# Folding the Fourier branch of a token-mixing kernel about the middle of each segment, with its norm in channel-major form and a new order of steps

## The chip, the core and the metric

The kernel is one program on one core of a Trainium2 chip. Its engines are TensorE (PE, matrix products, with PEld its weight loads), VectorE (DVE), ScalarE (ACT), GpSimd (POOL) and SyncE (SP, which issues transfers). The metric is the time of one execution on the device, in microseconds; lower is better.

## The reference

A two-layer block over 512 latent tokens and 256 context tokens of width 1024. Each layer has a token-mixing stage and a SwiGLU stage, each followed by a modulated residual and a layer norm. The mixing stage projects the tokens to three head groups: group A (512 channels, a bidirectional linear recurrence with a GELU gate), group B (256 channels, chunked spatial gating) and group C (256 channels in four heads of 64), which is the Fourier branch that this case is about. Context tokens are a segment of their own, of 256 positions.

```python
def fourier_mix(xf, wf):
    Bsz, L, _ = xf.shape
    z = xf.reshape(Bsz, L, H_C, HEAD_DIM).astype(jnp.float32)
    f = jnp.fft.fft2(z, axes=(1, 3), norm="ortho").real
    return jnp.einsum("blhc,hce->blhe", f, wf.astype(jnp.float32)).reshape(Bsz, L, D_C).astype(xf.dtype)
...
    y = jnp.concatenate([rms_norm(y_a, g_mix[:D_A]),
                         rms_norm(y_b, g_mix[D_A:D_A + D_B]),
                         rms_norm(y_c, g_mix[D_A + D_B:])], -1)
    return y @ w_out
```

The real part of the transform is C z cos - S z sin, with the position matrices C and S on the left and the channel matrices on the right. The last layer needs latent tokens only.

## The kernel before

Tokens lie in tiles of 128: two of context, four of latents (the second layer mixes the four alone). Channel-major buffers hold 128 channels by up to 768 tokens. All large products run on float32r operands: `split` makes a high part on ACT (L208) and a low part by a subtraction (L203) on an engine that the caller chooses, and `mm` multiplies high by high, high by low and low by high, three products in a row on PE. All products are issued by one line, L134. Plain float32 products appear in the profile as two records each.

Weights come in units of mostly 1024 columns (512 KB) in a written order, loaded ahead by SP and split ahead of use; the subtraction of a unit goes to `wsub`, which is POOL at a mixing stage's start and becomes DVE at the letter D of the stage's string; it keeps its value in the MLP that follows. In the MLP PE makes the up projections of one tile of hidden channels after another (L1234 and L1235 in the profile) and, after 4 or 5 of these, the down projection of the group for every token tile; its residual sum ends in an addition on POOL.

The mixing stage follows a string of letters, STEPS, and PE's order is bound to it (`pe.fixed`). Letters that matter here: Z and z load and compute the Fourier input projection (`fourier_in`, split by L877 on ACT and L878 on DVE), c is the column transform (`fourier_cols`), e, p and s are the gates and scans of the recurrence, whose activations fill ACT (L822 to L833), V, v, U, u and t are the spatial gating, g is a gate of group A, m a block of the modulation of later stages (`mod`, with copies at L522), R the rows of the gate, L lets the held GELUs go, a digit sets a memory reserve, D is as above.

After the string, the function `mixing` puts group B's rows (`put_group`: transposes to channel-major), sums group A's squares over channels by products with a column of ones, makes a reciprocal root (`rstd`: DVE, then a power on POOL, L232) and a diagonal matrix from it on DVE (L1172). Then `fourier` computes the positions: for each token tile the products of the full position matrices (units dftc, k_cosl and k_sinl, 4.5 MB over the two layers) with the transformed columns, token-major, a copy and `rms` on ACT and DVE, and a tile later the transposes by `put_group`. Before tile BETWEEN the spread of group A's roots (products with a matrix of ones) and its scaling come in between. The output projection follows, and its layer norm.

## Time and profile before

| | us |
|---|---|
| median of 3 runs | 1506.51 (1502.71 to 1507.05) |
| the profiled execution | 1506.1 |
| its span | 1504.1 |
| PE busy in the span | 1416.7 |
| DVE, ACT, POOL busy | 893.4, 551.7, 294.8 |

From about 60 to 352 us the first layer mixes tokens, up to 860 us its MLP runs; from there to 1139 us the second layer mixes, its MLP ends at 1487 us. A row of the timeline gives the start, the duration, the instruction and, in brackets, the idle time in front of it with the engine and tile that ended it. Ends of products are modelled, so two rows' distance from start to start is the better measure of what products cost.

### The profile page before, as it was taken

What the parts mean: (1) busy time and instruction counts of PE and PEld (TensorE: products, weight loads), DVE (VectorE), ACT (ScalarE), POOL (GpSimd) and SP (SyncE); (2) the same over time, 40 slices, a digit from 0 to 9 for tenths busy, and PEclk for the clock granted to TensorE, in tenths of its full rate; (3) what the DMA queues carried; (4) which work ended last, traced back from release to release, by engine and by line L of the source; (5) the groups of instructions that cost most, each with busy time, mean ns of one, the idle gap of its engine ahead of it and who ended that gap; (6) DMA issues with size and microseconds to landing.
All of it is one profiled execution on the core that took longest, in us unless ns stands there. A gap on an engine that the chain in (4) does not pass through costs nothing.

```text
span 1504.1 us, 18734 instructions
## 1 busy us (share of the span) xinstructions
PE 1416.7 (94%) x7527; PEld 1197.2 (80%) x7527; DVE 893.4 (59%) x1259; ACT 551.7 (37%) x784; POOL 294.8 (20%) x190
## 2 busy tenths in 40 slices
PE   6999888999999999999999998959998999999997
PEld 3788756779888888888888878858777888888885
DVE  6749756779527439443527396688788343353427
ACT  4576445345312202111203146886536232322210
POOL 3303323230021030030030044223230111020201
PEclk9999999999999999999999999969999999999999
DMA  9503365317116216244127004015427352242201
GB/s 329 139 15 99 105 224 186 97 31 236 43 43 211 70 55 198 71 139 162 36 77 231 28 29 128 1 48 169 127 67 228 98 154 71 70 130 60 77 14 56
DMA packets 169430, 163.56 MB, mean 109 GB/s; under 512 B 10456, under 2 KB 126648, under 8 KB 169344
## 3 DMA queue, kind: packets, MB, share of 16 engines
q1 hardware_dynamic: 169232, 162.08, 34.4%
q8 instruction: 59, 0.97, 0.3%
q0 software_dynamic: 112, 0.30, 0.1%
q14 instruction: 27, 0.22, 0.0%
HBM read 160.25 MB, written 2.10 MB: 108 GB/s over the span
## 4 chain that ended last, share of the span: by engine, by line
PE 72%; DVE 12%; ACT 5%; issue 3%; DMA 3%; POOL 3%; SPq 2%; DVEq 0%; POOLq 0%; ACTq 0%
PE mm L134 67%; PE aux L134 5%; POOL smalls L232 2%; DVE f L678 1%; DVE f L203 1%; DVE f L1220 1%; DMA f<-in_w_in_dram 1%; DVE r L203 1%; SPq L1315 1%; POOL r L203 1%; SPq L1333 1%; DVE f L832 1%; DVE smalls L709 1%; ACT r L208 1%; DVE f L835 1%
## 5 line engine op out<-in xcount | busy, mean ns | idle before, releaser
L134 PE MATMUL mm<-r,r 128*128 128x512 f32 (+1 forms) x6192 | 1230.6, 360 | 21.0 <-DVE f L1220 7.3
L134 PEld LDWEIGHTS mm<-r,r 128*128 128x128 f32 x6192 | 1035.7, 191 | 202.0 <-DVE f L1220 12.5
L208 ACT ACTIVATE r<-f 128x1024 fp32r<-128x1024 f32 (+2 forms) x244 | 227.1, 951 | 578.0 <-PE mm L134 267.9
L203 DVE TENSOR_TENSOR r<-f,r 128x1024 fp32r<-128x1024 f32 (+3 forms) x245 | 266.8, 1111 | 133.8 <-ACT r L208 119.9
L203 POOL TENSOR_TENSOR f<-f,f 128x1024 f32<-128x1024 f32 (+2 forms) x44 | 109.7, 2493 | 654.3 <-DVE f L1220 479.3
L1220 DVE TENSOR_TENSOR f<-mm,f 128x512 f32<-128x512 f32 (+1 forms) x80 | 76.2, 952 | 145.2 <-PE mm L134 145.1
L203 POOL TENSOR_TENSOR r<-f,r 128x1024 fp32r<-128x1024 f32 (+2 forms) x59 | 107.0, 1823 | 226.0 <-ACT r L208 159.3
L1235 DVE TENSOR_TENSOR f<-mm,f 128x768 f32<-128x768 f32 (+1 forms) x44 | 36.2, 823 | 176.0 <-PE mm L134 176.0
L134 PE MATMUL aux<-r,r 128*128 128x256 f32 (+1 forms) x780 | 112.5, 306 | 25.3 <-DVE r L878 10.7
L134 PEld LDWEIGHTS aux<-r,r 128*128 128x128 f32 x780 | 106.5, 211 | 32.5 <-DVE r L878 12.7
L232 POOL TENSOR_TENSOR smalls<-smalls,neghalf 128x1 f32<-128x1 f32 (+2 forms) x69 | 67.2, 975 | 255.1 <-DVE smalls L231 245.7
L573 DVE SCALAR_TENSOR_TENSOR f<-f,stc,f 128x512 f32<-128x512 f32 x140 | 102.3, 762 | 2.8 <-DMA f<-in_w_mod_dram 1.3
L203 DVE TENSOR_TENSOR f<-f,f 128x512 f32<-128x512 f32 (+1 forms) x66 | 61.7, 939 | 9.8 <-ACT f L801 8.1
L1234 ACT ACTIVATE f<-mm 128x768 f32<-128x768 f32 (+1 forms) x44 | 30.7, 699 | 95.7 <-PE mm L134 95.7
L134 PE MATMUL aux<-cst,f 128*128 128x128 f32 (+2 forms) x259 | 38.7, 282 | 25.1 <-ACT f L644 8.7
L659 ACT ACTIVATE f<-aux,modT 128x128 f32<-128x128 f32 x128 | 48.5, 466 | 33.3 <-PE aux L134 33.3
L134 PEld LDWEIGHTS aux<-cst,f 128*128 128x128 f32 (+2 forms) x259 | 29.7, 143 | 37.3 <-ACT f L644 11.5
L644 ACT ACTIVATE f<-f,smalls 128x1024 f32<-128x1024 f32 x19 | 23.6, 1242 | 90.8 <-DVE smalls L643 90.8
L777 DVE SCALAR_TENSOR_TENSOR f<-mm,par,f 128x255 f32<-128x255 f32 (+3 forms) x48 | 26.1, 605 | 17.4 <-ACT f L771 17.4
L623 DVE BATCH_NORM_STATS2 smalls<-f 128x6 f32<-128x512 f32 x44 | 28.4, 682 | 5.0 <-DMA f<-in_ctx_dram 4.6
L801 ACT ACTIVATE f<-mm,par 128x768 f32<-128x768 f32 x32 | 28.0, 903 | 6.5 <-PE mm L134 5.0
L832 DVE SCALAR_TENSOR_TENSOR f<-f,f 128x768 f32<-128x768 f32 x16 | 22.2, 1390 | 12.7 <-ACT f L831 12.7
(117 smaller groups left out, 628.3 us busy)
## 6 DMA issues: line engine op xcount, KB each, us to landing
f<-in_w_mod_dram SPq DMA_DIRECT2D x96, 512.0 KB
f<-in_w_up_dram SPq DMA_DIRECT2D x88, 512.0 KB
f<-in_w_down_dram SPq DMA_DIRECT2D x40, 512.0 KB
f<-in_w_in_dram SPq DMA_DIRECT2D x28, 512.0 KB
f<-in_w_out_dram SPq DMA_DIRECT2D x16, 512.0 KB
f<-in_b_mod_dram SPq DMA_DIRECT2D x6, 512.0 KB
f<-in_x_dram SPq DMA_DIRECT2D x4, 512.0 KB
f<-in_k_cosl_dram SPq DMA_DIRECT2D x4, 512.0 KB
```

The source lines that it names most:

```text
L134: i = f(*args, **kw)
L203: return eng.tensor_tensor(out=out, in0=a, in1=b, op=op)
L208: i = self.nc.scalar.activation(h, src, AF.Copy)
L232: self.nc.gpsimd.tensor_tensor(out=out, in0=v, in1=self.neghalf[:, 0:n], op=ALU.pow)
L573: nc.vector.scalar_tensor_tensor(out=b.f, in0=w, scalar=c, in1=b.f, op0=ALU.mult, op1=ALU.add)
L623: nc.vector.bn_stats(out=st[:, c, :], in_=x[:, c * 512 : (c + 1) * 512])
L659: nc.scalar.activation(y.f[:, q * P : (q + 1) * P], ps[:, q * P : (q + 1) * P], AF.Identity, bias=self.modT[:, slot, k, s : s + 1], scale= ...
L801: insts.append(nc.scalar.activation(g.f, ps[:, 256:1024], AF.Sigmoid, bias=par[:, col : col + 1]))
L832: nc.vector.scalar_tensor_tensor(out=t_.f, in0=r.f, scalar=1.0, in1=t_.f, op0=ALU.add, op1=ALU.mult)
L1220: self.nc.vector.tensor_tensor(out=tb.f, in0=ps[:, c], in1=m[:, c], op=ALU.mult)
L1234: nc.scalar.activation(g.f, pg[:, 256 + lo : 1024], AF.Silu)
L1235: nc.vector.tensor_tensor(out=g.f, in0=pu[:, 256 + lo : 1024], in1=g.f, op=ALU.mult)
```

## The change

The Fourier input is folded: for a segment of n positions, position k and its mirror n - k are added for the cosine and subtracted for the sine (`fourier_in`: a copy on ACT, two DVE operations per segment that read the projection backwards, then the split). The row in the middle is handled by itself (`fourier_middle`, six products of 2 columns). A column transform takes one pair of folded tiles (`fourier_cols`: 12 products of 128 columns). `fourier_positions` then works channel-major with the transformed columns as the stationary operand and half matrices as the moving one: for half the outputs, 12 products of 130 columns for the context and 24 of 258 for the latents; two DVE operations per half write the sum and, backwards, the difference. The norm is that of group A: squares, column sums by products with ones (`rms_rows`), a diagonal, now made on POOL for both, and a spread by products with ones (`rms_put`). One unit dft0 or dft1 of 1680 columns replaces the position matrices. New letters: F positions, A and N the sums of group A and of the Fourier group, B and Q their spreads, P group B's put, O sets `wsub` to POOL, H and h send the high part of units to POOL or ACT. The strings put these in a new order.

```diff
-BETWEEN = 2
-STEPS = ("feaekZeeppzssz6ssgpgpsssVvvsvUuuumgmcLccw7RmtgmmmD", "faeekeeZpsspszzcsppVcssvvgULusDsugwgtg")
+STEPS = ("feaekZeeppzssz8mOsshgpgss6p7VsshvUv6uvDcLmu8F6gHDc8cFwhuNRmtgDmAQmBmP", "faeekeepZsspszzsLpcpVcswF6gvUsOusvguhNsggtA7BPQ")
...
+    def segments(self, tiles):
+        return ([(0, NC_T * P)] if tiles[0] == 0 else []) + [(NC_T * P, NL_T * P)]
+    def fourier_in(self, u, tiles):
+        lo = tiles[0] * P
         pz = self.chan_proj(u, lo)
         self.drop(u)
+        z = self.buf(TOK)
+        self.nc.scalar.activation(z.f[:, lo:], pz[:, 256 + lo : 1024], AF.Copy)
+        for s, n in self.segments(tiles):
+            h = n // 2
+            mirror = pz[:, 256 + s + n - 1 : 256 + s + h : -1]
+            self.nc.vector.tensor_tensor(out=z.f[:, s + h + 1 : s + n], in0=z.f[:, s + 1 : s + h], in1=mirror, op=ALU.subtract)
+            self.nc.vector.tensor_tensor(out=z.f[:, s + 1 : s + h], in0=z.f[:, s + 1 : s + h], in1=mirror, op=ALU.add)
         zt = (self.buf(TOK), self.buf(TOK))
+        self.split(zt[0].r[:, lo:], zt[1].r[:, lo:], z.f[:, lo:])
+        z.free()
         return zt
+    def fourier_middle(self, tiles, bd, zt):
+        ps = self.psum_aux()
+        at = slice(128, 513, 384) if tiles[0] == 0 else slice(512, 514)
+        for k in range(2):
+            self.mm(ps[:, 2 * k : 2 * k + 2], tuple(b.r[:, k * 256 : k * 256 + P] for b in bd), tuple(b.r[:, at] for b in zt[k]), True, True)
+        self.nc.vector.tensor_copy(self.middle, ps[:, 0:4])
+        return 1 if tiles[0] == 0 else 0
+    def fourier_cols(self, at, bd, zt):
+        zc = (self.buf(512), self.buf(512))
+        ps = self.psum_aux()
+        for c in range(2):
+            for k in range(2):
+                o = ps[:, c * 256 + k * P : c * 256 + (k + 1) * P]
+                self.mm(o, tuple(b.r[:, at[c] : at[c] + P] for b in zt[k]), tuple(b.r[:, k * 256 + c * P : k * 256 + (c + 1) * P] for b in bd), True, True)
+        self.split_psum(*(b.r for b in zc), ps)
+        return zc
+    def fourier_positions(self, i, n, u, zc, y, sq):
+        nc = self.nc
+        h = n // 2
+        o, s = (0, 0) if n == NC_T * P else (DFT_CTX, NC_T * P)
+        w, nj = h + 2, h // P
+        for k in range(2):
+            ps = self.psum_big()
+            for c in range(2):
+                for j in range(nj):
+                    mat = slice(o + (c * nj + j) * w, o + (c * nj + j + 1) * w)
+                    e = slice(c * 256 + k * P, c * 256 + (k + 1) * P)
+                    self.mm(ps[:, c * 512 : c * 512 + w], tuple(b.r[:, e] for b in zc[j]), tuple(b.r[:, mat] for b in (u.high, u.low)), j == 0, j == nj - 1)
+            t = self.buf(w)
+            sign = u.low.f[:, DFT_ALT + (0 if n == NC_T * P else 130) :][:, 0:w]
+            m = 2 * k + (0 if s == 0 else self.middle_at)
+            nc.vector.scalar_tensor_tensor(out=t.f, in0=sign, scalar=self.middle[:, m : m + 1], in1=ps[:, 0:w], op0=ALU.mult, op1=ALU.add)
+            nc.vector.tensor_tensor(out=y[k].f[:, s : s + h + 1], in0=t.f[:, 0 : h + 1], in1=ps[:, 512 : 512 + h + 1], op=ALU.add)
+            nc.vector.tensor_tensor(out=y[k].f[:, s + n - 1 : s + h : -1], in0=t.f[:, 1:h], in1=ps[:, 513 : 512 + h], op=ALU.subtract)
+            t.free()
+            nc.scalar.activation(sq[k].f[:, s : s + n], y[k].f[:, s : s + n], AF.Square)
+        for pair in zc:
+            for b in pair:
+                b.free()
+    def rms_rows(self, tiles, sq, width):
+        nc = self.nc
+        n_t = len(tiles)
+        ssum = self.psum_aux()
         for n, ti in enumerate(tiles):
+            for i, b in enumerate(sq):
+                self.pe.matmul(ssum[:, n : n + 1], b.f[:, ti * P : (ti + 1) * P], self.ones[:, 0:1], start=i == 0, stop=i == len(sq) - 1)
+        for b in sq:
+            b.free()
+        r = self.small(n_t)
+        self.rstd(r, ssum[:, 0:n_t], 1.0 / width, EPS)
+        dg = self.buf(n_t * P)
+        for n in range(n_t):
+            nc.gpsimd.tensor_scalar(out=dg.f[:, n * P : (n + 1) * P], in0=self.ident, scalar1=r[:, n : n + 1], scalar2=None, op0=ALU.mult)
+        return dg
+    def rms_put(self, tiles, dg, ys, k0):
+        nc = self.nc
+        lo = tiles[0] * P
+        pr = self.psum_big()
+        for n, ti in enumerate(tiles):
+            self.pe.matmul(pr[:, 256 + ti * P : 256 + (ti + 1) * P], self.ones, dg.f[:, n * P : (n + 1) * P], start=True, stop=True)
+        dg.free()
+        for m, y in enumerate(ys):
+            nc.vector.tensor_tensor(out=y.f[:, lo:], in0=pr[:, 256 + lo : 1024], in1=y.f[:, lo:], op=ALU.mult)
+            for a, b in ((0, NC_T), (NC_T, NT)):
+                if a >= tiles[0]:
+                    H, L = (x[:, :, k0 + m, :] for x in self.XT(a, b))
+                    src = y.f[:, a * P : b * P].rearrange("p (t n) -> p t n", n=P)
+                    nc.scalar.activation(H, src, AF.Copy)
+                    self.tt(nc.gpsimd if k0 + m in (0, 2) else nc.vector, L, src, H.bitcast(F32), ALU.subtract)
             y.free()
...
+                if self.middle_at is None:
+                    self.middle_at = self.fourier_middle(tiles, bd, zt)
+                zc.append(self.fourier_cols(folded.pop(0), bd, zt))
+                if not folded:
                     for b in bd + [b for pair in zt for b in pair]:
+                        b.free()
+            elif x == "F":
+                if not fu:
+                    fu.append(self.use(f"dft{l}"))
+                    yf.extend([self.buf(TOK), self.buf(TOK)])
+                    qf.extend([self.buf(TOK), self.buf(TOK)])
+                n = segs.pop(0)[1]
+                nj = n // 2 // P
+                assert len(zc) >= nj
+                self.fourier_positions(l, n, fu[0], zc[:nj], yf, qf)
+                del zc[:nj]
+                if not segs:
+                    self.drop(fu[0])
+            elif x == "A":
+                assert len(sq) == MA and not self.late
+                diag["A"] = self.rms_rows(tiles, sq[:1], D_A)
+            elif x == "N":
+                assert not segs
+                diag["N"] = self.rms_rows(tiles, qf, 256)
+            elif x in "BQP":
+                assert len(sq) == MA and len(cv) == MA and len(uv["u"]) == len(uv["v"]) == n_t // 2 and len(zt) == 2
+                if x == "B":
+                    self.rms_put(tiles, diag.pop("A"), [hs[m] for m in range(MA)], 0)
+                elif x == "Q":
+                    self.rms_put(tiles, diag.pop("N"), yf, 6)
+                else:
+                    assert gated
+                    for n, b in enumerate(uv["u"]):
+                        self.put_group(b.f, tiles[2 * n], 4)
                         b.free()
...
+            elif x == "O":
+                self.wsub = nc.gpsimd
+            elif x in "Hh":
+                self.weng = "pool" if x == "H" else "act"
...
-            for nm in ("k_cosl", "k_sinl"):
-                for q in range(2):
-                    us.append(Unit(f"{nm}{l}.{q}", 1024, dma(t[nm][:, q * 1024 : (q + 1) * 1024], "p n -> p n")))
+            a = DFT_CTX if l == DEPTH - 1 else 0
+
+            def load(b):
+                nc.sync.dma_start(out=b[:, a:], in_=t["k_dft"][:, a:])
+
+            def parts(u):
+                self.split(u.high.r[:, a:DFT_ALT], u.low.r[:, a:DFT_ALT], u.low.f[:, a:DFT_ALT], self.weng, self.wsub)
+            us.append(Unit(f"dft{l}", DFT_COLS, load, scale=parts))
```

Not shown are the removed bodies of the old functions, a branch of `split` that makes high parts on POOL, checks, and the constants' tables.

First place, PE at the end of the first mixing stage. The first piece is of the kernel before: the transposes of group B's puts (cst is the identity), group A's sums, and the first products of the positions (the moving operand is named first, the stationary one second: r_512 are the transformed columns, r_1024 the matrices of dftc).

```order
L134 MATMUL aux<-cst,f_512_1414 128x128 x4
L134 MATMUL aux<-cst,f_512_1465 128x128 x4
L134 MATMUL aux<-cst,f_512_1516 128x128 x4
L134 MATMUL aux<-ones,f_768_1100 128x1 x6
L134 MATMUL aux<-r_512_1610,r_1024_1943 128x256
L134 MATMUL aux<-r_512_1611,r_1024_1943 128x256
L134 MATMUL aux<-r_512_1610,r_1024_453 128x256
L134 MATMUL aux<-r_512_1621,r_1024_1943 128x256
```

In the changed kernel the positions have been computed earlier, and the same place reads so: two modulation blocks (f, stc) with group A's sums, the spread of the Fourier group and a modulation block's transposes (cst) between them.

```order
L137 MATMUL aux<-f_1024_1741,stc 32x512 x2
L137 MATMUL aux<-f_1024_1850,stc 32x512 x2
L137 MATMUL aux<-f_1024_1852,stc 32x512 x2
L137 MATMUL aux<-f_1024_129,stc 32x512 x2
L137 MATMUL aux<-ones,f_768_1120 128x1 x6
L137 MATMUL mm<-f_768_1817,ones 128x128 x6
L137 MATMUL aux<-cst,f_512_1525 128x128 x4
L137 MATMUL aux<-f_1024_1217,stc 32x512 x2
L137 MATMUL aux<-f_1024_1734,stc 32x512 x2
```

The long row of position products has left this place; sums and a spread stand between the modulation blocks.

Second place, PE in the second mixing stage behind the Fourier input projection. Before, the last products of the column transform (r_768 the projection, r_512 the maps) are followed by the input products of the spatial gating (r_1024 its weights, r_4096 the tokens).

```order
L134 MATMUL aux<-r_512_6538,r_768_7428 128x2x128
L134 MATMUL aux<-r_512_7284,r_768_4115 128x2x128
L134 MATMUL aux<-r_512_7284,r_768_7603 128x2x128
L134 MATMUL aux<-r_512_6538,r_768_7603 128x2x128
L134 MATMUL aux<-r_512_7284,r_768_7604 128x2x128
L134 MATMUL aux<-r_1024_7510,r_4096_77 128x256
L134 MATMUL aux<-r_1024_5292,r_4096_77 128x256
L134 MATMUL aux<-r_1024_7510,r_4096_79 128x256
```

In the changed kernel transposes of the spatial gating's maps and the position products (r_1680 is the unit dft1) come next.

```order
L137 MATMUL aux<-r_512_655,r_768_5456 128x128
L137 MATMUL aux<-r_512_7210,r_768_5456 128x128
L137 MATMUL aux<-r_512_655,r_768_5327 128x128
L137 MATMUL aux<-cst,f_512_7038 128x128 x4
L137 MATMUL mm<-r_1680_7584,r_512_7575 128x258
L137 MATMUL mm<-r_1680_7585,r_512_7575 128x258
L137 MATMUL mm<-r_1680_7584,r_512_7576 128x258
L137 MATMUL mm<-r_1680_7584,r_512_7601 128x258
```

The positions moved from the stage's end to directly behind the column transform, in front of the spatial gating's input.

Third place, POOL at the start of the last MLP. Before, after the roots of the layer norm (smalls), only the residual additions (f_1024_72 to f_1024_75 are the latents).

```order
L232 TENSOR_TENSOR smalls<-smalls,neghalf 128x1 x2
L203 TENSOR_TENSOR f_1024_72<-f_1024_72,f_1024_71 128x1024
L203 TENSOR_TENSOR f_1024_73<-f_1024_73,f_1024_9264 128x1024
L203 TENSOR_TENSOR f_1024_74<-f_1024_74,f_1024_8788 128x1024
L203 TENSOR_TENSOR f_1024_75<-f_1024_75,f_1024_8790 128x1024
L203 TENSOR_TENSOR f_1024_72<-f_1024_72,f_1024_70 128x1024
L203 TENSOR_TENSOR f_1024_73<-f_1024_73,f_1024_111 128x1024
```

In the changed kernel subtractions of weight blocks (r_1024 from f_1024) stand between them.

```order
L206 TENSOR_TENSOR r_1024_8947<-f_1024_8816,r_1024_7769 128x1024
L206 TENSOR_TENSOR r_1024_9024<-f_1024_114,r_1024_8853 128x1024
L206 TENSOR_TENSOR r_1024_9021<-f_1024_112,r_1024_8860 128x1024
L206 TENSOR_TENSOR r_1024_8214<-f_1024_8869,r_1024_8217 128x1024
L206 TENSOR_TENSOR r_1024_2146<-f_1024_192,r_1024_4474 128x1024
L206 TENSOR_TENSOR f_1024_72<-f_1024_72,f_1024_8018 128x1024
L206 TENSOR_TENSOR f_1024_73<-f_1024_73,f_1024_3771 128x1024
L206 TENSOR_TENSOR f_1024_74<-f_1024_74,f_1024_8618 128x1024
L206 TENSOR_TENSOR r_1024_6460<-f_1024_6207,r_1024_8187 128x1024
L206 TENSOR_TENSOR r_1024_6193<-f_1024_5953,r_1024_7197 128x1024
```

POOL has these subtractions throughout this MLP, where DVE had them before.

## Rows read from the trace of the kernel before

**Rows 1.** Page, head and part 1: busy time, share, instructions.

```profile
span 1504.1 us, 18734 instructions
...
PE 1416.7 (94%) x7527; PEld 1197.2 (80%) x7527; DVE 893.4 (59%) x1259; ACT 551.7 (37%) x784; POOL 294.8 (20%) x190
```

**Rows 2.** Page, part 4: the last chain by engine.

```profile
PE 72%; DVE 12%; ACT 5%; issue 3%; DMA 3%; POOL 3%; SPq 2%; DVEq 0%; POOLq 0%; ACTq 0%
```

**Rows 3.** Stretches: from:to, length, busy us by engine, then granted clock, DMA, GB/s.

```profile
core 0: us, PE busy (x) PEld busy (x) DVE busy (x) ACT busy (x) POOL busy (x), PEclk, DMA share, GB/s
196.00:270.00 74.00, 61.44 (x378) 44.85 (x377) 45.46 (x93) 37.57 (x77) 23.29 (x22) 0.93 0.65 219
241.70:245.10 3.40, 3.40 (x18) 3.40 (x17) 1.51 (x9) 0.89 (x3) 1.89 (x2) 0.50 0.39 159
352.00:860.00 508.00, 508.00 (x2785) 442.91 (x2784) 261.39 (x333) 111.85 (x130) 62.20 (x25) 1.00 0.35 110
977.00:1001.00 24.00, 7.80 (x29) 6.13 (x29) 20.68 (x26) 23.06 (x29) 2.44 (x2) 0.61 0.20 61
1139.00:1487.00 348.00, 347.83 (x1559) 289.21 (x1560) 154.64 (x163) 92.24 (x116) 43.33 (x18) 1.00 0.30 89
```

**Rows 4.** Timeline of PE, end of the first mixing stage: start, us, row, idle before.

```profile
194.72 1.77 PE L134 MATMUL aux<-r,r 128*128 128x256 f32 x12
197.12 0.98 PE L134 MATMUL aux<-r,r 128*128 128x256 f32 x6 [0.62 <-DVE r L878]
...
200.73 0.97 PE L134 MATMUL aux<-r,r 128*128 128x256 f32 x6 [0.24 <-DVE r L878]
...
227.24 0.66 PE L134 MATMUL aux<-cst,f 128*128 128x128 f32 x4 [0.96 <-ACT f L522]
...
231.91 0.66 PE L134 MATMUL aux<-cst,f 128*128 128x128 f32 x4 [2.16 <-ACT f L522]
...
235.22 1.60 PE L134 MATMUL aux<-cst,f 128*128 128x128 f32 x12 [0.80 <-ACT f L522]
238.20 0.65 PE L134 MATMUL aux<-cst,f 128*128 128x128 f32 x4 [1.38 <-DVE r L874]
238.80 1.50 PE L134 MATMUL aux<-ones,f 128*128 128x1 f32 x12
240.70 4.63 PE L134 MATMUL aux<-r,r 128*128 128x256 f32 x24 [0.40 <-DVE r L874]
...
245.81 1.50 PE L134 MATMUL mm<-f,ones 128*128 128x128 f32 x12
247.07 3.12 PE L134 MATMUL aux<-r,r 128*128 128x256 f32 x24
250.03 0.38 PE L134 MATMUL aux<-cst,f 128*128 128x128 f32 x2
```

**Rows 5.** Timeline of PE, second mixing stage.

```profile
984.65 0.80 PE L134 MATMUL aux<-r,r 128*128 128x256 f32 x2 [6.76 <-ACT r L877]
...
1000.69 14.21 PE L134 MATMUL aux<-r,r 128*128 128x256 f32 x96 [6.10 <-DVE r L878]
...
1031.72 5.64 PE L134 MATMUL mm<-r,r 128*128 128x512 f32 x24
...
1057.31 1.68 PE L134 MATMUL aux<-ones,f 128*128 128x1 f32 x8 [2.10 <-DVE f L203]
1058.85 8.39 PE L134 MATMUL aux<-r,r 128*128 128x256 f32 x48
```

**Rows 6.** Page, part 5: weight loads in front of the products into aux.

```profile
L134 PEld LDWEIGHTS aux<-r,r 128*128 128x128 f32 x780 | 106.5, 211 | 32.5 <-DVE r L878 12.7
```

**Rows 7.** Timeline of ACT, second mixing stage.

```profile
984.02 1.07 ACT L877 ACTIVATE r<-mm 128x512 fp32r<-128x512 f32 x2
...
997.45 1.99 ACT L208 ACTIVATE r<-f 128x1024 fp32r<-128x1024 f32 x2
999.34 1.06 ACT L877 ACTIVATE r<-aux 128x512 fp32r<-128x512 f32 x2
```

**Rows 8.** Groups by line and form in the last MLP (1139 to 1487 us).

```profile
L203 DVE TENSOR_TENSOR r<-f,r 128x1024 fp32r<-128x1024 f32 x60 | 81.9, 1390 | 57.5 <-ACT r L208 57.3
L208 ACT ACTIVATE r<-f 128x1024 fp32r<-128x1024 f32 x60 | 62.0, 1057 | 137.9 <-PE mm L134 89.2 <-POOL f L203 39.3 <-PE aux L134 5.3
L203 POOL TENSOR_TENSOR f<-f,f 128x1024 f32<-128x1024 f32 x16 | 41.8, 2614 | 252.9 <-DVE f L1220 188.4 <-issue 59.7 <-DMA f<-in_w_up_dram 4.8
```

**Rows 9.** Timeline of POOL, last MLP.

```profile
1207.06 2.39 POOL L203 TENSOR_TENSOR f<-f,f 128x1024 f32<-128x1024 f32 x1 [3.56 <-DVE f L1220]
1212.57 3.34 POOL L203 TENSOR_TENSOR f<-f,f 128x1024 f32<-128x1024 f32 x1 [3.12 <-DVE f L1220]
```

**Rows 10.** Timeline of DVE, last MLP.

```profile
1178.53 1.82 DVE L203 TENSOR_TENSOR r<-f,r 128x1024 fp32r<-128x1024 f32 x2 [0.19 <-ACT r L208]
...
1212.43 6.83 DVE L203 TENSOR_TENSOR r<-f,r 128x1024 fp32r<-128x1024 f32 x4
```

More of the change, by code (lines that the diff above doesn't have):

```diff
@@ L317, in consts @@
         self.spl = cp.tile([P, 2, 8], F32, tag="spl", name="spl")
+        self.middle = cp.tile([P, 4], F32, tag="middle", name="middle")
     def XT(self, a, b):
@@ L923, in fourier @@
-    def fourier(self, l, tiles, zc, between):
-        ctx_too = tiles[0] == 0
-        zcv = [tuple(b.r.rearrange("p (c n) -> p c n", c=2) for b in pair) for pair in zc]
-        late = []
-        def positions(mat, base, cnt):
-            for m in range(cnt):
-                if base + m == BETWEEN:
-                    between()
-                ps = self.psum_aux()
-                for c in range(2):
-                    for j in range(cnt):
-                        self.mm(
-                            ps[:, 0:256], mat(c, j, m), tuple(x[:, c, :] for x in zcv[base + j]),
-                            c == 0 and j == 0, c == 1 and j == cnt - 1,
-                        )
-                y = self.buf(256)
-                self.nc.scalar.activation(y.f, ps[:, 0:256], AF.Copy)
-                self.rms(y.f)
-                late.append((y, tiles[base + m]))
-                if len(late) > 1:
-                    put()
-            for pair in zc[base : base + cnt]:
-                for b in pair:
-                    b.free()
-        def put():
-            y, ti = late.pop(0)
-            self.put_group(y.f, ti, 6)
-            y.free()
-        if ctx_too:
-            uc = self.use("dftc")
-            positions(lambda c, j, m: tuple(b.r[:, c * 512 + j * 256 + m * P : c * 512 + j * 256 + (m + 1) * P] for b in (uc.high, uc.low)), 0, NC_T)
-            self.drop(uc)
-        us = self.use_all([f"{nm}{l}.{q}" for nm in ("k_cosl", "k_sinl") for q in range(2)])
-        def mat(c, j, m):
-            u = us[2 * c + j // 2]
-            o = (j % 2) * 512 + m * P
-            return (u.high.r[:, o : o + P], u.low.r[:, o : o + P])
-        positions(mat, NC_T if ctx_too else 0, NL_T)
-        for u in us:
-            self.drop(u)
-        return put
@@ L1063, in mixing @@
         zt, zc, uv, ws = [], [], {"v": [], "u": []}, []
+        segs, yf, qf, fu = self.segments(tiles), [], [], []
+        folded = [(s + j * P, s + n // 2 + j * P) for s, n in segs for j in range(n // 2 // P)]
+        self.middle_at = None
+        diag, gated = {}, []
         m2b, rows = gate_rows or ([], [])
@@ L1134, in step @@
             elif x == "t":
+                assert not self.late and len(uv["u"]) == len(uv["v"]) == n_t // 2 and ws
                 self.gating(tiles, uv["u"], vb, ws)
+                gated.append(1)
             elif x == "L":
@@ L1157, in mixing @@
             step(x)
[L1158 removed]
+        assert "".join(sorted(set(STEPS[l]) & set("ABNQPtFL"))) == "ABFLNPQt" and not diag and not segs and not work and not self.late
         mod()
[L1160 to L1191 removed]
         self.reserve = 7000
[L1194 removed]
         self.pe.fixed = False
@@ L1422, in plan @@
                     spatial(l)
+                elif x == "F" and us[-1].name != f"dft{l}" and f"dft{l}" not in [u.name for u in us]:
+                    dft(l)
                 elif x in "UV":
@@ L1483, in shape_constants, with half, sign @@
     k_small = np.concatenate([ident, np.kron(np.eye(2), c64) / 8.0, np.kron(np.eye(2), s64) / 8.0], 1)
-    def tiles(a):
-        return a.reshape(-1, P, a.shape[1]).transpose(1, 0, 2).reshape(P, -1)
-    cl, sl = dft(SEQ)
-    cc, sc = dft(CTX)
-    k_dftc = np.concatenate([tiles(cc), -tiles(sc)], 1) / np.sqrt(CTX)
+    def half(n):
+        a = 2.0 * np.pi * (np.outer(np.arange(n // 2), np.arange(n // 2 + 2)) % n) / n
+        both = [np.cos(a), -np.sin(a) * (np.arange(n // 2 + 2) < n // 2)]
+        return np.concatenate([m.reshape(-1, P, n // 2 + 2).transpose(1, 0, 2).reshape(P, -1) for m in both], 1) / np.sqrt(n)
+    def sign(n):
+        return np.ones((P, 1)) * (1.0 - 2.0 * (np.arange(n // 2 + 2) % 2)) / np.sqrt(n)
     quarter = D // 4
```

58 lines of the change are left out of this document (7 added, 51 removed).

## The prediction

> **What bounds the kernel now.** I read the page first. TensorE (PE) is busy for 1416.7 us of a 1504.1 us span [rows 1] and carries 72% of the chain of work that ended last [rows 2]. The execution took 1506.1 us, 2.0 us more than its span; the median of the runs is 1506.51 us, so a change of the span may be taken off either. Then the table of stretches, since a mean over the program says little: in both MLP stages PE has no free time (508.00 us of 508, 347.83 of 348), so nothing there can give time back. Its idle time lies in the mixing stages: 12.6 us of the 74 us at the end of the first, 16.2 of the 24 us from 977 us on in the second [rows 3]. Last I read PE's timeline in those two places, for what it does and which wait ends last. At the end of the first stage the column transform has short waits on its own splits, the modulation blocks wait for one another (0.96, 2.16, 0.80, 1.38 us), and then PE computes the Fourier positions from 240.70 us on with almost no wait [rows 4]. In the second it waits 6.76 us for ScalarE (ACT) and 6.10 us for VectorE (DVE) around the column transform, and works through the positions from 1058.85 us on [rows 5]. So work removed from the positions is time, if nothing late takes its place; work removed near 977 us is not.
>
> **The change, part by part.** *Positions.* Before, a context tile takes 12 products and a latent tile 24, each 256 columns wide: 2 x 12 + 4 x 24 = 120 in the first layer, 96 in the second. Afterwards they are 12 of 130 columns and 24 of 258, and in the second layer 24 of 258. An undisturbed run of 24 goes from 247.07 to 250.03 us, 0.123 us each [rows 4]. At that price 84 fewer products are 10.3 us, and 72 fewer are 8.9 us. The first 24 of the first layer took 4.63 us, since PE's clock was granted at 0.50 there, the lower of its two levels, from 241.70 us on [rows 3]; such a stretch may fall elsewhere afterwards, which is worth 1.7 us.
>
> *Column transform.* 36 products of 256 columns become 36 of 128 (24 and 24 in the second layer), with 6 of 2 columns in front for the middle rows. No row of before has a product of this kind narrower than 256 columns. On the cheap side the nearest are twelve transposes of 128 columns, 1.60 us, beside twelve products of 256 columns, 1.77 us [rows 4]: 0.014 us each. On the dear side stand the 128 x 1 sums on plain float32, 1.50 us for six, 0.25 us each [rows 4]. I take the cheap end, since the weight load in front of each product has the same 128 columns at any width and takes 0.21 us, longer than the spacing of the products [rows 6]: 36 x 0.014 less, and 6 x 0.1 more for the middle rows, comes to +0.1 us. At the dear end the 48 narrow products of the first layer (12 of the positions among them) cost 0.13 us more each, 6 us. In the second layer both lie in the stretch that waits for ACT anyway, so neither end counts.
>
> The Trainium skill (TensorE: Matmul & The Clock Gate, Back-to-back issue gap) has a sustained spacing that falls with the columns, to about 81 ns at 128. By it the 36 products would be an estimated 1.5 us cheaper than I count. The rows show nearly the same spacing at 128 and 256 columns, so I go by them.
>
> *The norm.* The per-tile path (square, reciprocal root, scale, two transposes per tile) goes; its transposes cost PE 0.2 us a tile beside the work around them, 1.3 us for six tiles and 0.9 us for four [rows 4]. In come 12 sums and 6 spreading products in the first layer, 8 and 4 in the second, at 0.25 us each (six spreads too take 1.50 us): 4.5 and 3.0 us. Net 3.2 us and 2.1 us more. Group A's sums and spreads stand in both kernels.
>
> *Work of PE:* -10.3 + 3.2 + 0.1 = -7.0 us and -8.9 + 2.1 = -6.8 us.
>
> *Waits of the first layer.* The modulation blocks at the end now have sums, spreads or group puts between them, some 1.5 us each, about what each waits for ACT now [rows 4]; of their 5.3 us I take 2 us as gone. Pairs of the column transform are now followed at once by the positions that read them, so a wait for a split, 0.54 us on ACT [rows 7] and as much again on DVE, replaces the five waits of 0.19 to 0.62 us, 1.55 us together: nothing gained. The new chain of sums, root, diagonal and spread goes over DVE, POOL, POOL and PE; the spread stands one modulation block (some 2.5 us) or less behind its sums, and I allow 1 us of wait. Together -1 us.
>
> *Waits of the second layer.* The fold sits between the input projection and the split: an ACT copy, two DVE operations and the split again, on a stretch where ACT has other work queued. The split of the projection began at 984.02 us there and the last split of the columns at 999.34 us, each behind activations of the scans or splits of weights [rows 7]. PE waits there as before; the spatial gating's input products, which it reached at 1000.69 us, come behind the positions (24 products, 3 us), which come behind the same splits. The 2.10 us in front of group A's sums [rows 5] goes to some other place of the end. I count these as equal.
>
> *POOL takes the subtractions of weights.* The second string has O and after it no D, so each weight block split after it, and throughout the last MLP, has its low part made on POOL: some 60 operations that take DVE 81.9 us in that stretch, on a POOL that has 41.8 us of residual additions there [rows 8]. POOL takes 2.39 us for such an operation, 3.34 us when DVE subtracts beside it [rows 9]. 60 x 2.39 + 41.8 = 185 us, 60 x 3.34 + 41.8 = 242 us, of 348: there is room on average, and a block is split at least one block ahead, 24 products that take 5.64 us [rows 5]. I cost it at nothing in the MLP, covered by those products. At the end of the mixing stage POOL also makes the reciprocal roots, each of which may now stand behind a subtraction that is running; one operation of 2.4 us is what I take as uncovered: +2 us (bounds 0 and 5, two operations).
>
> The rows speak against this move too: four subtractions on DVE took 6.83 us while one of POOL's lay beside them, where two alone take 1.82 us, so 3.2 us more, against POOL's 3.34 us [rows 9, 10]. The Trainium skill (SBUF — State Buffer, Terms: shared port pair) says that such operations of DVE and GpSimd exclude each other for a whole instruction; the trace agrees. It is the ground of rival D.
>
> **Sum.** -7.0 - 6.8 - 1 + 2 = -12.8 us; with most of the 1.7 us of the slow stretch on the first positions -14 us. 1506.1 - 14 = **1492 us**.
>
> **Rivals.** *Less waiting as well (B):* ACT and DVE lose the per-tile norm, so the waits of [rows 4] and the 16.2 us near 977 us shrink too. Against it: what is late there is the scans' activations, which stay. If the modulation waits go entirely (3.3 us more), the 2.10 us too, and 8 of the 16 us: 1492 - 13 = 1479 us. *Narrow products are dear (C):* 6 us for the 48 narrow ones, and 5 us at the two ends, because sums, roots and diagonals stand in one chain: 1503 us. *POOL is late in the last MLP (D):* POOL serves in order, and a residual addition that waits for the products of a tile holds up every subtraction behind it. This decides once the queue is longer than the 5.64 us of a block's products: two operations of 3.34 us are. One wait of 4 us in each of the 5 groups is 20 us: 1512 us, slower than before. For it: ACT's high parts already wait 39.3 us for POOL's additions in that stretch [rows 8]; against: the mean load of 53 to 70%.
>
> **How the numbers follow.** Forecast (A, 1484 to 1500): 0.53. B: 0.17. C (1500 to 1507): 0.14. D: 0.16. About 0.3%, 4.5 us, is what a measurement of this kernel can tell. A and B are faster, and a fourth of C; the rest of C is the same; nearly all of D slower: 0.74, 0.11, 0.15. The range 1475 to 1508 holds A, C, most of B and the start of D; A by itself is 1484 to 1500.
>
> **What would show it.** The profile afterwards should show 128-column products of the column transform at some 0.12 us and the positions as 258-column rows; PE's busy time some 14 us lower, in the mixing stages only; the last MLP with no PE idle and POOL busy for 185 to 242 us in it. The wait near 977 us should be there still, for ACT and DVE. The prediction is wrong if PE waits for POOL in the last MLP, if the narrow products take 0.25 us, or if the ends of the two stages show new waits for POOL's roots and diagonals of more than 5 us.

## The result, and the profile after

The changed kernel takes 1521.89 us (median of 4, 1519.35 to 1523.32), the kernel before 1504.61 us: a ratio of 1.0115, 95% interval 1.0087 to 1.0143. It is slower by 1.2%, where 0.9% faster was forecast, and lies above the range. The profiled execution has a span of 1520.4 us, 16.3 us more than before.

The page of the changed kernel, parts 1 and 5 [rows 1]: PE's busy time fell by 8.8 us, POOL's rose by 169 us, and the subtractions on POOL that make low parts, most of them of weights, went from 59 to 126.

```profile
span 1520.4 us, 18534 instructions
PE 1407.9 (93%) x7423; PEld 1189.1 (78%) x7423; DVE 836.6 (55%) x1184; ACT 539.9 (36%) x744; POOL 463.9 (31%) x269
...
L206 POOL TENSOR_TENSOR r<-f,r 128x1024 fp32r<-128x1024 f32 (+2 forms) x126 | 269.8, 2160 | 266.3 <-ACT r L211 134.6
```

The stretches of the changed kernel, columns as in [rows 3]; the last one begins when the last MLP is under way:

```profile
196.00:270.00 74.00, 67.71 (x410) 51.11 (x409) 48.91 (x86) 30.43 (x54) 23.37 (x26) 0.98 0.68 228
977.00:1001.00 24.00, 6.37 (x28) 6.11 (x28) 21.30 (x22) 15.20 (x19) 8.49 (x3) 0.53 0.08 22
1057.00:1080.00 23.00, 9.26 (x39) 7.52 (x37) 13.41 (x23) 9.72 (x18) 15.17 (x13) 0.65 0.15 48
1160.00:1503.00 343.00, 342.88 (x1533) 284.41 (x1534) 94.43 (x102) 85.72 (x107) 184.72 (x79) 1.00 0.29 85
```

The end of the first mixing stage is denser than before (67.7 us of 74 busy, 61.4 before). The last MLP is as dense as ever, 342.88 us of 343, with POOL busy for 184.7 us in it. What is new is in the second mixing stage: 9.3 us busy of the 23 us from 1057 us on, where it was 22.3 us. The kernel before, same columns:

```profile
1057.00:1080.00 23.00, 22.29 (x139) 20.54 (x140) 15.11 (x29) 12.96 (x27) 7.11 (x7) 0.85 0.36 106
```

PE at the end of the first stage, timeline of the changed kernel [rows 4]:

```profile
196.34 2.79 PE L137 MATMUL aux<-r,r 128*128 128x128 f32 x24
...
200.49 3.13 PE L137 MATMUL mm<-r,r 128*128 128x258 f32 x22 [0.22 <-DVE r L884]
...
209.65 2.74 PE L137 MATMUL aux<-ones,f 128*128 128x1 f32 x24
...
230.43 1.92 PE L137 MATMUL aux<-f,stc 128*32 128x512 f32 x16
233.92 1.47 PE L137 MATMUL aux<-ones,f 128*128 128x1 f32 x12 [1.56 <-DVE f L206]
235.25 1.58 PE L137 MATMUL mm<-f,ones 128*128 128x128 f32 x12
```

24 products of 128 columns take 2.79 us, 0.116 us each: the cheap price. The 12 sums of the Fourier norm (24 records) take 2.74 us, 0.23 us each, and of the waits between modulation blocks one of 1.56 us is left, in front of group A's sums, with two of 0.5 to 0.6 us in front of the spread.

PE in the second stage, timeline of the changed kernel [rows 5]:

```profile
960.56 14.29 PE L137 MATMUL mm<-r,r 128*128 128x256 f32 x66 [0.90 <-ACT f L807]
987.42 0.37 PE L137 MATMUL aux<-r,r 128*128 128x2 f32 x1 [12.57 <-ACT r L211]
992.91 0.59 PE L137 MATMUL aux<-r,r 128*128 128x2 f32 x2 [5.12 <-DVE r L206]
...
1068.92 0.98 PE L137 MATMUL aux<-r,r 128*128 128x256 f32 x3 [9.32 <-DVE f L1072]
...
1075.86 2.54 PE L137 MATMUL mm<-f,ones 128*128 128x128 f32 x8 [3.25 <-POOL f L992]
```

Three new waits: 12.57 us where it was 6.76, 9.32 us and 3.25 us. DVE and POOL around the first of them, two timelines of the changed kernel:

```profile
974.44 0.95 DVE L841 TENSOR_TENSOR f<-f,f 128x768 f32<-128x768 f32 x1
...
976.17 0.68 DVE L845 TENSOR_TENSOR_SCAN f<-f,f 128x256 f32<-128x256 f32 x1
...
983.51 2.80 DVE L841 TENSOR_TENSOR f<-f,f 128x768 f32<-128x768 f32 x1
986.24 0.41 DVE L927 TENSOR_TENSOR f<-f,mm 128x255 f32<-128x255 f32 x1
986.57 2.50 DVE L845 TENSOR_TENSOR_SCAN f<-f,f 128x256 f32<-128x256 f32 x1
989.10 3.18 DVE L846 TENSOR_TENSOR_SCAN f<-f,f,f 128x512 f32<-128x512 f32 x1
992.20 0.66 DVE L206 TENSOR_TENSOR r<-f,r 128x512 fp32r<-128x512 f32 x1
```

```profile
982.71 8.49 POOL L206 TENSOR_TENSOR r<-f,r 128x1032 fp32r<-128x1032 f32 x3 [20.52 <-ACT r L211]
...
1053.60 1.71 POOL L237 TENSOR_TENSOR smalls<-smalls,neghalf 128x4 f32<-128x4 f32 x1 [2.89 <-DVE smalls L236]
1055.41 6.22 POOL L992 TENSOR_SCALAR f<-cst,smalls 128x128 f32<-128x128 f32 x4
1061.60 2.34 POOL L206 TENSOR_TENSOR r<-f,r 128x1024 fp32r<-128x1024 f32 x1
1063.90 1.26 POOL L206 TENSOR_TENSOR f<-f,f 128x512 f32<-128x512 f32 x1
```

While POOL subtracts for 8.49 us, three DVE operations take 2.80, 2.50 and 3.18 us; the first two forms take 0.95 and 0.68 us a few rows earlier. Behind them stands the fold's last subtraction, for which PE waits. The Trainium skill (SBUF — State Buffer, Terms: shared port pair) has the loser block for the whole instruction. The excess of the first two, 1.85 and 1.82 us, agrees with it: it stays within one operation of POOL, 2.83 us. The second wait is a queue: the root, four diagonals, a subtraction of weights and a sum of squares follow one another on POOL until 1065.16 us. ACT then waits for POOL and DVE for ACT, as their rows (timelines of the changed kernel) say, and the evictions of the gating (L1072), which PE waits for, stand behind that in DVE's queue:

```profile
1065.19 1.15 ACT L1402 ACTIVATE r<-f,par 128x1024 fp32r<-128x1024 f32 x1 [3.28 <-POOL f L206]
```

```profile
1066.37 1.28 DVE L1403 SCALAR_TENSOR_TENSOR r<-f,par,r 128x1024 fp32r<-128x1024 f32 x1 [5.13 <-ACT r L1402]
1067.57 0.69 DVE L1126 TENSOR_TENSOR f<-f,f 128x512 f32<-128x512 f32 x1
1068.17 0.86 DVE L1072 SCALAR_TENSOR_TENSOR f<-aux,par,f 128x128 f32<-128x128 f32 x3
```

### The profile page after: what moved, and what is told of

Its sections match the earlier page's. It is cut to its first block, busy times and chain, and to the rows that moved or that the text cites. A ratio compares the mean times of both kernels' runs of the same rounds, so it can differ in the third digit from the quotient of the medians.

```text
span 1520.4 us, 18534 instructions
## 1 busy us (share of the span) xinstructions
PE 1407.9 (93%) x7423; PEld 1189.1 (78%) x7423; DVE 836.6 (55%) x1184; ACT 539.9 (36%) x744; POOL 463.9 (31%) x269
## 4 chain that ended last, share of the span: by engine, by line
PE 68%; DVE 14%; POOL 5%; ACT 5%; issue 5%; DMA 2%; SPq 1%; DVEq 0%; POOLq 0%; ACTq 0%
PE mm L137 65%; PE aux L137 3%; POOL smalls L237 2%; DVE r L206 2%; POOL r L206 2%; DVE f L206 1%; DMA f<-in_w_mod_dram 1%; POOL f L992 1%; DVE f L684 1%; ACT f L665 1%; DVE f L1269 1%; DVE f L841 1%; ACT r L211 1%; DVE f L840 1%; DVE smalls L629 1%
## 5 line engine op out<-in xcount | busy, mean ns | idle before, releaser
L137 PE MATMUL mm<-r,r 128*128 128x512 f32 (+2 forms) x6252 | 1245.3, 360 | 31.5 <-DVE f L1269 7.0
L211 ACT ACTIVATE r<-f 128x1024 fp32r<-128x1024 f32 (+3 forms) x241 | 223.1, 946 | 607.6 <-PE mm L137 223.2
L206 POOL TENSOR_TENSOR r<-f,r 128x1024 fp32r<-128x1024 f32 (+2 forms) x126 | 269.8, 2160 | 266.3 <-ACT r L211 134.6
L206 DVE TENSOR_TENSOR r<-f,r 128x1024 fp32r<-128x1024 f32 (+4 forms) x181 | 196.8, 1102 | 100.0 <-ACT r L211 75.5
L237 POOL TENSOR_TENSOR smalls<-smalls,neghalf 128x1 f32<-128x1 f32 (+3 forms) x61 | 62.6, 1028 | 234.8 <-DVE smalls L236 228.8
L579 DVE SCALAR_TENSOR_TENSOR f<-f,stc,f 128x512 f32<-128x512 f32 x140 | 112.5, 826 | 13.9 <-DMA f<-in_w_mod_dram 11.9
L137 PE MATMUL aux<-r,r 128*128 128x256 f32 (+2 forms) x576 | 80.3, 300 | 37.7 <-ACT r L211 14.3
L137 PEld LDWEIGHTS aux<-r,r 128*128 128x128 f32 x576 | 77.0, 207 | 42.6 <-ACT r L211 14.8
L137 PE MATMUL aux<-cst,f 128*128 128x128 f32 (+1 forms) x239 | 35.3, 284 | 25.4 <-ACT f L650 8.7
L1283 ACT ACTIVATE f<-mm 128x768 f32<-128x768 f32 (+1 forms) x44 | 30.5, 694 | 75.0 <-PE mm L137 75.0
L137 PEld LDWEIGHTS aux<-cst,f 128*128 128x128 f32 (+1 forms) x239 | 27.7, 144 | 34.0 <-ACT f L650 11.1
L683 DVE SCALAR_TENSOR_TENSOR f<-f,smalls,f 128x1024 f32<-128x1024 f32 (+1 forms) x24 | 28.2, 1190 | 0.0
```

The costliest lines, as they stand in the source:

```text
L137: i = f(*args, **kw)
L206: return eng.tensor_tensor(out=out, in0=a, in1=b, op=op)
L211: i = self.nc.scalar.activation(h, src, AF.Copy)
L237: self.nc.gpsimd.tensor_tensor(out=out, in0=v, in1=self.neghalf[:, 0:n], op=ALU.pow)
L579: nc.vector.scalar_tensor_tensor(out=b.f, in0=w, scalar=c, in1=b.f, op0=ALU.mult, op1=ALU.add)
L683: nc.vector.scalar_tensor_tensor(out=n.f[:, c], in0=x[:, c], scalar=mu, in1=g[:, c], op0=ALU.subtract, op1=ALU.mult)
```

## The experiments

Theory P: the second stage loses its time to POOL's subtractions and diagonals. Theory S: to the new order of its steps and the fold's longer chain. Two measures serve below: the ratio to the kernel before, and two parts of the profiled span, divided where the products of the second layer's Fourier input projection end (for the changed kernel the row at 960.56: 960.56 + 14.29 = 974.85 us, and 1520.4 - 974.85 = 545.6 us after it). The expectations use the stretch from the start of the last SiLU of the first MLP to the load of the activation's table in front of the first of the second: 296.1 us before, 321.3 us in the changed kernel. The second part repeats well: 527.3, 529.0 and 527.5 us in the three runs of the changed kernel with D first in the second string and no O (e3 and the two of e10). The first part does not: the nine runs whose first layer is the changed kernel's reach its MLP's first SiLU anywhere from 346.4 to 350.9 us, so a few us there say little.

**The engine alone (four runs).** e7 removes D from the second string of the kernel before; e3 puts it first in that of the changed kernel.

```diff
-... "faeekeeZpsspszzcsppVcssvvgULusDsugwgtg"
+... "faeekeeZpsspszzcsppVcssvvgULussugwgtg"
...
-... "faeekeepZsspszzsLpcpVcswF6gvUsOusvguhNsggtA7BPQ"
+... "DfaeekeepZsspszzsLpcpVcswF6gvUsusvguhNsggtA7BPQ"
```

> The kernel before with the D taken out of the second layer's string, so that POOL keeps the subtractions of weights from there on, and nothing else changed. Theory P: 8 us or more slower than before, 1513 us or more. Theory S: the last MLP's 2.4 us and little else, some 1507 us.

> The changed kernel with the letter D put at the start of the second layer's string and its O taken out, so that all subtractions of weights from the second mixing stage on are DVE's. Theory P: the 8.5 us block of three POOL subtractions at 983 us goes and with it some 6 us of the waits around the column transform, the two queues at the end lose 5 us or more and the last MLP 2.4 us: some 1508 us. Theory S: only the last MLP's 2.4 us come back, some 1519 us.

Measured: e7 1.0106 (1.0084 to 1.0128), e3 0.9943 (0.9924 to 0.9962). One letter in the old kernel costs as much as the whole change, and D first in the changed kernel gains 24 us, 10 us more than theory P said. Of e7's loss 10.9 us lie between the projection and the last MLP's first SiLU, and 6.1 us behind that, where PE waits once for POOL:

```profile
1181.53 12.32 PE L134 MATMUL mm<-r,r 128*128 128x512 f32 x46 [3.54 <-POOL r L203]
```

e6 gives the changed kernel the old order in its second layer, with POOL; e2 has the diagonals on DVE (`nc.vector.tensor_scalar` in `rms_rows`).

```diff
-... "faeekeepZsspszzsLpcpVcswF6gvUsOusvguhNsggtA7BPQ"
+... "faeekeeZpsspszzcsppVcssvvgULussugwgtgPAFNBQ"
```

> The changed kernel with the second layer's steps in the order of the kernel before (the positions and the norms at the end), and POOL keeping all subtractions of weights (no D). Theory P: POOL is as late as in the changed kernel, only the place differs; some 1515 to 1522 us. Theory S: the 25 us that the second mixing stage lost come back but for the last MLP's 2.4 us: some 1496 to 1500 us.

> The changed kernel with the diagonals of rms_rows on DVE again, all else as in the changed kernel. Theory P (POOL: the second mixing stage loses its time to subtractions of weights and diagonals on POOL, which hold up one another and DVE): the 9.3 us wait at 1059 us and the 3.3 us wait at 1072.6 us go for the larger part, 8 us, so some 1514 us. Theory S (the new order of steps and the longer fold chain cost it, POOL is a bystander): at most 2 us, some 1520 us.

Measured: e6 1.0092 (1.0071 to 1.0114), e2 1.0130 (1.0104 to 1.0156). Theory S falls as the main cause: as long as POOL subtracts, the old order shows no clear difference (the intervals of e6 and of the changed kernel overlap). Of theory P the part on the diagonals falls too: on DVE they gain nothing, and the wait for L1072 stays, 10.43 us. In e3, where the four diagonals take POOL 6.21 us as before but no subtraction of weights follows them, it is 3.03 us.

**Where in the stage (three runs).** e1 has D in place of O (POOL subtracts up to the gating), e11 has D first and keeps O (POOL from there on), e12 has D in front of zz and O behind F, which moves the three subtractions of the 8.49 us block alone.

> The changed kernel with D in place of O in the second layer's string: POOL subtracts around the column transform as in the changed kernel, DVE from the gating on. The 24.4 us that came back with all of them on DVE are split here. If the queue behind the 8.5 us block at 983 us is the larger part (the wait there, and the half clock after it), some 1512 us; if the queues at the end of the stage (the 9.3 us wait and those behind it) are, some 1504 us.

> The complement of the run with D in place of O: D at the start of the second layer's string, O at its place, so POOL subtracts only from the gating on. If the two parts add up, the second mixing stage is 11 us longer than with all on DVE (296.2 us by the SiLU marks) and the whole takes a ratio of 1.0015 to the kernel before, some 1508 us; if POOL is late only when both lie together, under 1502 us.

> The changed kernel with a D in front of the letters zz and the O behind F, so that only three subtractions of the second layer move from POOL to DVE: those of the 8.5 us block at 983 us. If DVE's fold waits for exactly these, the waits around the column transform shrink by 6 to 8 us and the ratio to the kernel before falls from 1.0115 to 1.006 or 1.007 (about 1514 us); if the time that early subtractions on POOL cost (14 us by the stretches of the run with D in place of O) is spread over many places, 1520 us.

Measured: e1 1.0023 (1.0007 to 1.0039), e11 1.0034 (1.0019 to 1.0049), e12 1.0094 (1.0071 to 1.0117). After the projection the parts are 527.3 us (e3), 535.0 (e1), 538.9 (e11) and 545.6 us (changed kernel): 7.7 + 11.6 against 18.3 us, nearly additive. The block moved by e12 is worth 3.2 us there (542.4 us), not 6 to 8, and its interval overlaps that of the changed kernel: without it ACT's queue still holds PE for some 11 us, so the cost is spread over many places. In front of the projection's end the changed kernel is 8.1 us later than e3 (974.85 against 966.79 us). Of these, 6.4 us lie between the last SiLU of the first MLP and that end (139.1 against 132.7 us); the other 1.7 us lie in the first mixing stage, where the two run the same program. In e1 the D stands about where the kernel before has it. So by the ratios the missing D is 0.9% of the time, some 14 us, and with a D there the change still gains nothing.

**The fold without POOL (nine runs).** e9 and e15 are the kernel before with DVE for all subtractions, in the second stage and in both; e10 is the changed kernel with D first in both strings and no O or D later.

> The kernel before with its D at the start of the second layer's string, so that it too makes all subtractions of weights on DVE. If POOL's subtractions cost the old kernel as much as the changed one in the early part (14 us), some 1492 us, and the fold would be worth nothing in the second layer; if the old order hid them, within 3 us of the kernel before, and the rest is the fold's longer chain.

> The changed kernel with all subtractions of weights of both mixing stages on DVE (D at the start of both strings, no O or later D). If what was seen in the second layer holds in the first as well, where POOL subtracts for part of the stage, another 5 us less than with D in the second alone (1497.5 us): a ratio under 0.991. If the first layer's stretches were chosen where POOL is free, the same or slower, since DVE is the busier engine there (65 of 75 us from 121 us on): 0.994 or more.

> The kernel before with all subtractions of weights of both mixing stages on DVE (D at the start of both strings, none later): the like of the changed kernel with D in both (ratio 0.9922), without the fold. If the fold is worth its products (PE work of 7 us in each layer) like for like, this run lies 10 to 14 us above that one: 1502 to 1506 us (0.998 to 1.001). If the second stage's 288.5 us of the old kernel with DVE were the fold's missing gain, they stay here: 1493 us (0.992) or less. If the second stage loses its 16 us here too, though no Fourier branch has changed, by the SiLU marks (304 us instead of 288.5), it is the order of the ends that any change upstream of them shifts.

> The changed kernel with D in both strings once more, on the same chip as its like without the fold: 1491 to 1496 us, a ratio of 0.992 to 0.994.

Measured: e9 0.9968 (0.9952 to 0.9983), e10 0.9922 (0.9897 to 0.9946), and on one chip e15 0.9990 (0.9979 to 1.0002) with e10 again at 0.9903 (0.9881 to 0.9925), 1492.3 us. By this pair the change is worth 0.9%, 12 to 13 us (medians 1504.47 and 1492.31 us). But D at the start of the first string does not suit the old kernel: its first MLP's first SiLU comes at 369.2 us, against 363.4 to 365.2 us in the three runs without it, while the changed kernel has it at 340.8 us, against 346.4 to 350.9 us. Against e9, the fastest form of the kernel before that was run, e10 gains 0.5% on the same chip, 8 us (1499.92 to 1491.73 us). e10 is the fastest version that was run.

e14 has the fold in the first layer alone and the second layer of e9; e13 is that with the first string of e10.

> The Fourier branch folded in the first layer alone, with the changed kernel's string there; the second layer has the Fourier branch and the order of the kernel before, with its D at the start. The like run with the fold in both layers and D at the start of the second took 1497.5 us. By the SiLU marks the second mixing stage is 7.7 us longer with the fold than without when DVE subtracts in both. If the fold's chain and place cost that, some 1488 us (ratio 0.988); if the 6.6 us that are lost before the Fourier input projection come from the first layer's change (the products around the last normalisation of the first MLP stand in another order in all runs with the fold), some 1495 us (0.993).

> As the run with the fold in the first layer alone, and all subtractions of weights on DVE in the first mixing stage too, which gave 7 us there by the SiLU marks with the fold in both. If it adds up: 7 us less than that run, 1481 us (0.983); if the 3 us that the second stage gave back then come again, 1484 us.

Measured: e14 0.9987 (0.9973 to 1.0002), e13 0.9954 (0.9940 to 0.9969). Neither expectation holds: e14 is no faster than the kernel before. After the projection e9 has 523.1 us, e14 532.8 us with the same second layer, and e3, with fold and new order there too, 527.3 us. So 9.7 us are lost in a layer whose code did not change; e15 with 523.1 us and e13 with 533.2 us say the same. In front of the projection it is the same: from the last SiLU of the first MLP to the projection's end e9 takes 126.1 us, e14 134.1 us, e13 134.0 us and e3 132.7 us. There PE waits for ACT in the last normalisation of the first MLP, 2.1 us in all in e9 and 6.7 us in e14, e13 and e3. So this loss comes with the changed first layer, whatever the second. Behind the projection the largest wait of e14 stands in the last normalisation of the second mixing stage. PE's row in e9, then in e14:

```profile
1129.62 0.66 PE L134 MATMUL aux<-cst,f 128*128 128x128 f32 x4 [1.52 <-ACT f L644]
```

```profile
1133.00 1.97 PE L137 MATMUL aux<-cst,f 128*128 128x128 f32 x8 [7.91 <-ACT f L650]
```

DVE's rows show what stands in between. In e9 the normalisation's scaling comes first and the modulation sums of the next stage (L571, L573) behind it; in e14 sums (L577, L579) stand in front of the scaling. e9, then e14:

```profile
1121.21 1.28 DVE L677 SCALAR_TENSOR_TENSOR f<-f,smalls,f 128x1024 f32<-128x1024 f32 x1
...
1125.64 0.47 DVE L571 TENSOR_SCALAR f<-f,stc 128x512 f32<-128x512 f32 x1
```

```profile
1115.18 0.48 DVE L577 TENSOR_SCALAR f<-f,stc 128x512 f32<-128x512 f32 x1
1115.69 1.54 DVE L579 SCALAR_TENSOR_TENSOR f<-f,stc,f 128x512 f32<-128x512 f32 x2
...
1123.29 1.28 DVE L683 SCALAR_TENSOR_TENSOR f<-f,smalls,f 128x1024 f32<-128x1024 f32 x1
```

That order isn't in the strings. Why it came out otherwise here stays open; an order by hand there was not tried. The wait is not the same in every run of the changed kernel. It is 7.53 us in e8 (fold in both layers, old order, D first) and 3.01 us in e3:

```profile
1131.12 1.97 PE L137 MATMUL aux<-cst,f 128*128 128x128 f32 x8 [7.53 <-ACT f L650]
```

```profile
1125.42 1.09 PE L137 MATMUL aux<-cst,f 128*128 128x128 f32 x8 [3.01 <-ACT f L650]
```

So the 5.5 us from e14 to e3 are not the fold's alone: 4.9 us are this wait. With the fold and the old order (e8) the part after the projection takes 534.6 us, 1.8 us more than in e14. A gain of the fold by itself in the second layer is not shown.

The last three: the old order with D at its old place (e4), with D first (e8), and D first with the diagonals on DVE (e5).

> The changed kernel with the second layer's steps in the order of the kernel before, with the D at its old place (the run with this order and no D took 1520.3 us). If the subtractions of the end of the stage are what costs, some 1500 us; if those around the column transform are, 1512 us or more. An order that is better in itself would show as under 1494 us.

> As the run with the old order of the second layer's steps, but with D at the start, so that DVE makes all its subtractions of weights. With e3 it tells what the new order of the second layer is worth by itself: within 2 us of 1497.5 us if nothing; under 1494 us if the positions are better at the end of the stage, over 1501 us if they are better behind the column transform.

> All subtractions of weights of the second layer on DVE and the diagonals on DVE too (with POOL's subtractions left alone, that took 3.6 us more, not less). If POOL's diagonals (2.5 us for four, where DVE takes 0.8) are the 3.5 us wait in front of the spread of group A, 2 us less than the 1497.5 us: 1495.5 us. If that wait is the chain of sums, root and diagonal whatever makes it: 1497 us.

Measured: e4 1.0018 (1.0002 to 1.0034), e8 0.9993 (0.9974 to 1.0012), e5 0.9992 (0.9974 to 1.0009). With DVE subtracting, the new order (e3, 0.9943) beats the old one by 0.5%, though 4.5 of the 7.3 us after the projection are the wait shown above. The diagonals are better off on POOL by as much, which was not expected. 6.6 us of that lie in front of the projection (973.4 against 966.8 us). `rms_rows` serves both layers, so the edit moves the first layer's diagonals too: 5.2 us of them are already there when the first MLP's first SiLU starts (353.2 against 348.0 us), and e2, the other run with that edit, is the second latest there, at 352.3 us. What in the first stage loses them is not shown.

## Why the prediction was wrong

The spans, cut at the SiLUs and at the end of the second layer's Fourier input projection; the last column compares the two kernels with DVE subtracting in the second layer:

| us | forecast | before to changed | e9 to e3 |
|---|---|---|---|
| to the first SiLU of the first MLP | -8.0 | -13.7 | -17.2 |
| to its last SiLU | 0 | +2.4 | +2.3 |
| to the end of the projection | | +8.3 | +6.7 |
| to the first SiLU of the last MLP | -6.8 + 2 | +18.7 | +2.9 |
| to the end | 0 | +0.6 | +1.3 |
| the span | -12.8 | +16.3 | -4.0 |

The second layer's forecast stands in the fourth row and goes for the third and fourth together. The marks (starts of the rows of the SiLU, L1234 or L1283, and the projection's end) are 363.4, 847.1, 977.9 and 1146.0 us before, 349.7, 835.7, 974.9 and 1161.7 us in the changed kernel, 365.2, 848.9, 975.0 and 1140.0 us in e9, 348.0, 834.0, 966.8 and 1134.7 us in e3. Up to the first row's mark both columns compare the same two programs, since only the second string was edited, and still they differ by 3.5 us; so single rows are good to a few us.

- **The step that failed** is "POOL takes the subtractions of weights", sized +2 us with bounds 0 and 5, and with it "Waits of the second layer", counted as equal. Over the third and fourth rows POOL's subtractions cost the changed kernel 25.3 us (against e3) and the kernel before, which had a D, 7.8 us (against e9): 17.5 us net; the ratios give some 21 us. I had the rate (2.39 us, 3.34 us beside DVE) and the mutual blocking, but counted one operation at the end of the stage. POOL makes 21 subtractions of weights in that stage, ten more than before, and there are POOL queues all along it; DVE's rows stretch beside them, and ACT and PE wait for both. PE's idle time in the fourth row went from 28.0 to 48.9 us. One sign that the prediction named for being wrong came true, the 9.32 us at the end of the stage, though by e2 and e3 the diagonals are not its cause. The letter O has no part in it: `wsub` is POOL from the stage's start, and what counts is that no D follows.
- **Rival D** had the sign and, at 1512 us, a third of the loss, but the wrong place. In the last MLP POOL is busy for 184.7 us, as worked out (185), and PE waits for nothing; the price was paid in the mixing stage, in front of it. A wait for POOL in the last MLP occurs once in e7, 3.54 us.
- **The first layer** gained more than the 8.0 us forecast: 11.3 us by the last SiLU of its MLP, 8.6 us of PE's work and 2.7 us of its waits, where 7.0 and 1 were forecast. The MLP itself is 2.4 us longer, with 19 more products in it. That the projection of the second layer ends 8.2 us earlier (974.98 us in e9, 966.79 us in e3), nearly the forecast, is luck: 14.8 us were gained by the last SiLU and 6.7 us lost behind it. The cheap price of the narrow products held (0.116 us), so rival C falls. The Trainium skill's spacing of 81 ns at 128 columns (TensorE: Matmul & The Clock Gate, Back-to-back issue gap) is not what these products show.
- **The second layer without POOL** was forecast at -6.8 us of work and equal waits. From e9 to e3 the third and fourth rows give +9.5 us. In the fourth PE's busy time fell by 3.7 us only and its idle time rose by 6.6 us: the waits around the column transform are 19.8 us instead of 17.0, and one of 3.24 us for diagonals on POOL in front of a spread is new. The 6.7 us in the third row come with the changed first layer (e14, e13), through an order that the prediction did not consider; its cause stays open.
- **PE's work**: 13.8 us less was forecast for both layers; the page shows 8.8 us. Part of the difference is half clock: 0.53 was granted from 977 us on and 0.65 from 1057 us on, after waits, where the kernel before had 0.61 and 0.85.

## What to carry to other kernels

Moving work to an idle engine has to be costed at the moments when the busy engines wait for it, not by its share of a stage: POOL with 185 us of work in a dense MLP cost the changed kernel nothing, and with 21 subtractions in a stage of short chains 25 us. A setting that stays in force, such as `wsub`, should be followed to its next setting before anything else in a change is costed. Before a rewrite is judged, run the old kernel with the same setting: without its D it is as slow as the changed one, and each at the best setting that was run, the change gains 8 us. Cut the time at several marks, too: a part that agrees with the forecast may be a larger gain and a loss behind it.

## What the runs showed of the hardware

Scans on DVE stretch beside POOL's subtractions too: 128x256 from 0.68 to 2.50 us, 128x512 from 1.28 us (at 1056 us) to 3.18 us. Four 128x128 diagonals took POOL 6.22 us at 1055 us and 2.54 us at 1075 us, the first beside DVE's scans and scalings, which did not stretch there (a scan of 128x256 took 0.69 us).
